# A fourth pair of recurrent output tiles by seven quarter products, in a planned one-core kernel

## The chip, the cores and the metric

The kernel runs on one core of one Trainium2 chip. The metric is the device time of one launch in microseconds (us): the time before is the median of three runs. A core has five engines that matter here, each with a queue of its own that it works through in order: TensorE (PE in the profile, with its weight loads as PEld), VectorE (DVE), ScalarE (ACT), GpSimd (POOL) and SyncE (SP). SP issues nearly all plain transfers; GpSimd issues the accumulating ones, in which the data that arrive are added to what stands at the destination.

## What is computed

One layer of a hybrid mixer, 1024 tokens by 1024 channels, all in float32. The reference, cut to what matters:

```python
h = rmsnorm(x, norm_g) * (1 + scale) + shift          # shift, scale, gate from c
u = h @ w_in                                          # 1024 x 5120
cv, cg, cs, lx, ls = split(u)                         # five blocks of 1024 channels

v = causal_depthwise_conv(cv * sigmoid(cg), dw_w, dw_b)      # 31 taps
v = silu(layernorm(v, cln_g, cln_b))
y_conv = (v @ pw2_w + pw2_b) * silu(cs)

xs = causal_depthwise_conv(lx, sc_w, sc_b)                   # 4 taps
r, i = sigmoid(xs @ wr + br), sigmoid(xs @ wi + bi)          # block-diagonal, 8 heads of 128
a = exp(-8 * r * softplus(-lam))
hs = linear_scan(a, sqrt(1 - a * a) * i * xs)
y_lru = hs * silu(ls)

x = x + (1 + gate) * (concat(y_conv, y_lru) @ w_out)
out = rmsnorm(x, final_g)
```

The change is in one part of one product: `y_lru @ w_out[1024:]`, called "lru output" below.

## The kernel before

**Layout.** Channels lie on the 128 partitions, tokens along the free axis. A 1024-channel array is eight tiles of 128 x 1024; for `y_lru` a tile is one head.

**Products in three terms.** A float32 product is made from rounded parts. ScalarE casts an operand to a high part (`whi`, `yh`, `vh…`), VectorE, GpSimd or an accumulating transfer makes the low part (`wlo`, `yl`, `vl…`), and TensorE adds three terms: high by high (H), low input by high weight (X), high input by low weight (W). For an lru weight the low part is made by `remainder`: ScalarE writes the negated high part, and a transfer issued by GpSimd adds the weight from DRAM onto it.

**Quarter products.** The two later matrices (the pointwise `pw2` and the upper half of `w_out`) are multiplied as 2 x 2 blocks with seven block products in place of eight. The blocks are two output tiles by two halves of the tokens, and heads or channel tiles are taken in twos. The operands of the seven are blocks (A11, A12, A22 of the weight; B11, B21, B22 of the input) and sums of blocks (S1 to S4, T1 to T4). `quarters` makes the input's operands out of full tiles, with VectorE and ScalarE. `lru_pair` does this for a pair of lru output tiles over heads 0 to 3 (`JS = (0, 1)`, two twos), and adds heads 4 to 7 in the ordinary way. The order of its products is `LORDER = "p1zy2q3s4r"`: `p` is heads 4 to 7 of the first tile into the PSUM tile `lp`, `q` and `r` are the halves of heads 4 to 7 of the second tile, the others are the seven quarter products. PSUM tile `lx` is read out several times between its products. Before the change pairs 0, 1 and 2 are made so (`LRU_P = 3`), and output tiles 6 and 7 are plain: eight heads, three terms, two halves of 512 tokens, in PSUM tile `ps`.

**Sums of weights.** `lru_prepare` makes S1 to S4 of a pair early in the program, by loads, negated copies and accumulating loads into `lz`, splits them into `lh` and `ll`, and stores both in DRAM. `lru_pair` loads them back (`lsh`, `lsl`). `lru_sums` makes the T operands over heads 0 to 3 (`yhs`, `yls`).

**Results.** Each lru output tile is scaled by the gate into an `acc` tile and added to a copy of the input in DRAM (`accd`) by an accumulating transfer; `fin` loads it back in the last stage.

**The planner.** The program's order isn't written out. Every operation is handed to `Plan` with an engine, a cost, a priority and its reads and writes; `Plan.order` simulates the engines, and on each engine starts the ready operation of lowest priority number for which buffers are free. What comes out is a fixed order for each engine. Priorities count in slots: `n` goes up by one for each output tile, the lru output has slots 40 to 47, the pointwise stage starts at `C0 = 48`, the output stage at `D0 = 56`. The constants at the head of the file shift priorities.

**Buffers.** `big` is a pool of 47 tiles of 128 x 1024 float32, used for nearly everything. `raw`, `whi` and `wlo` are pools of two such tiles each, for weights. Where `w_bufs` is given "big", the high and low parts come from `big`; before the change all eight lru weights do (`LWB = "big"`). A convolution result that is ready long before the layer norm can be parked: `SPILL` names the tiles that `conv_sum` stores in DRAM (`cd`) and loads back (`cr`).

**Lines that the prediction touches.** L541 is the matmul of `mm_k` (plain tiles, and `p`, `q`, `r` of a pair), L1400 the matmul of the quarter products in `lru_pair`, L717 that of the pointwise and output stages, L386 and L394 ScalarE's casts and other operations, L405, L413 and L427 VectorE's (L413 also GpSimd's), L418 the accumulating transfers, L432 SP's transfers. Most are lines of helpers, so groups are told apart by the names of the tiles.

Of the kernel before, what the change touches and what calls it, by code (L numbers as in the profile page):

```python
# [14 lines left out]
P = 128  # L15
D = 1024
T = 1024
KT = D // P
# [28 lines left out]
UK = 7  # L47
HRES = 2
POOLED = (1, 3, 5)
TLATE = 2.5  # L50
QGATES = ((1, 5), (3, 0), (3, 2), (3, 4))
OUT_P = (0, 1, 2, 3)
HELD = (1, 2, 3)
# [23 lines left out]
NP = {0: (6, 0, 1), 512: (6, 0, 7), 768: (6, 0)}  # L77
SUMS = (2, 0, 4, 3, 1, 6, 7, 5)
CSD = 2
SPILL = (0,2,4)  # L80
SPP0, SPP1, SPN = 30, 40.5, 39
EVN = 4
CQR = 2
YHEADS, YSLOT = 2, 36
JS = (0, 1)
LRU_P = 3
NJ = len(JS)
LK = tuple(2 * j + z for z in (0, 1) for j in JS) + tuple(k for k in range(KT) if k // 2 not in JS)
LACT = ((0, 0), (0, 1), (1, 0), (1, 1))
LORDER = "p1zy2q3s4r"  # L90
LTP = 0.5
LTD = (2,1)
PREN, PRES = 5, 3
PREP, XCP = 18, 19
# [1 line left out]
XCN = 33  # L96
LEV = ()
LWB = "big"
LWO = 0.5
FINP = -0.5  # L100
BCLATE = False
BEHIND = 0
TERMS = {**{("pw2_0", c): ("HW", "X") for c in "1z"}, **{(f"out_{p}", "1"): ("HX", "W") for p in (0, 1, 2, 3)}, **{(f"pw2_{p}", "1"): ("HX", "W") for p in (1, 2, 3)}}
LTERMS = {}
LLATE = 45
SLOTT = {46: ("HX", "W"), 47: ("HX", "W")}
FINQ = 0.0
LRV = ()
# [48 lines left out]
class Plan:  # L157
# [14 lines left out]
    @staticmethod  # L172
    def keys(items):
        for it in items:
            if isinstance(it, tuple):
                yield it
            else:
                for i in range(it.parts):
                    yield (it, i)
# [162 lines left out]
def hymba_layer(ctx: ExitStack, tc: tile.TileContext, xT, vecs, mod_w, w_first, w_in,  # L342
# [37 lines left out]
    def ACT(prio, out, in_, func, n=T, bias=None, scale=None, accum=None, r=(), w=(),  # L380
            reserve=0, after=()):
        kw = {}

        def emit():
            if func == "copy":
                act.copy(out(), in_())  # L386
                return
            if bias is not None:
                kw["bias"] = bias
            if scale is not None:  # L390
                kw["scale"] = scale
            if accum is not None:
                kw["accum_out"] = accum
            act.activation(out=out(), in_=in_(), func=func, **kw)  # L394
        ptr = sum(x is not None and not isinstance(x, float) for x in (bias, scale))
        return S.op("ACT", a_cost(n, ptr) + (0.1 if accum is not None else 0), emit, prio, r, w,
                    table=SETS.get(func), reserve=reserve, after=after)
# [121 lines left out]
    def w_bufs(s, where=None):  # L519
        n = number[s]  # L520
        raw[s] = S.buf("raw", f"raw{n}", F32, KT)
        if where == "all":
            raw[s] = S.buf("big", f"raw{n}", F32, KT)
        whi[s] = S.buf("big" if where else "whi", f"whi{n}", F32R, KT)
        wlo[s] = S.buf("big" if where else "wlo", f"wlo{n}", F32R, KT)
# [285 lines left out]
    for i in range(IDLE):  # L811
        if i == IDLE0:
            for z in (0, 1):
# [3 lines left out]
             after=[spread_op] if i >= IDLE0 else [])  # L817
# [44 lines left out]
    for i, ld in enumerate(LOADS):  # L862
        p = due[ld] = i - 100.0
        k = int(ld[1])
# [4 lines left out]
        elif ld[0] in "wW":  # L869
            nk = 1 + (ld[0] == "W")  # L870
            rw, hi, lo = fw[k - k % 2]
# [492 lines left out]
    def lru_pair(p, n, use, firsts):  # L1364
        rest = LK[2 * NJ:]
        s0, s1 = ("lru", 2 * p), ("lru", 2 * p + 1)
        q = n - 1.4 - LWO
        for s in (s0, s1):
            w_bufs(s, LWB)
            DMA(n - 2.5 - LWO, k3(raw[s]), lambda s=s: wsrc(s)[:, :, :], FULL_BYTES, w=[raw[s]])  # L1370
        r0, r1 = raw[s0], raw[s1]
        for s, k in ((s0, 0), (s1, NJ)):
            hi, lo, r = whi[s], wlo[s], raw[s]
            cut = lambda b, k=k: (lambda: k3(b)()[:, k:, :])
            keys = lambda b, k=k: [(b, i) for i in range(k, KT)]
            ACT(q, cut(hi), cut(r), "copy", (KT - k) * P, r=keys(r), w=keys(hi))
            if s[1] in LRV:
                SUB(q, "DVE", cut(lo), cut(r), cut(hi), (KT - k) * P, r=keys(r) + keys(hi), w=keys(lo))
            else:
                remainder(q, cut(lo), cut(hi), lambda s=s, k=k: wsrc(s)[:, k:, :], (KT - k) * P, keys(hi), keys(lo))  # L1380
        def kk(b, i):
            return [(b, k) for k in range(i * NJ, i * NJ + NJ)]

        sh, sl = (big_buf(f"ls{h}{p}", F32R) for h in "hl")
        for h, t in zip("hl", (sh, sl)):
            DMA(n - 2.2, lambda t=t: t().bitcast(F32), lambda h=h: s_d[h, p], FULL_BYTES, r=[("ls", h, p)], w=[t], after=firsts)
        wq = {"S3": (sh, sl, 0, 0), "S4": (sh, sl, 1, 0), "S2": (sh, sl, 2, 0), "S1": (sh, sl, 3, 0),
              "A11": (whi[s0], wlo[s0], 0, None), "A12": (whi[s0], wlo[s0], 1, None),
              "A22": (whi[s1], wlo[s1], 1, None)}
        p0, x, y = mm_tile(f"lp{p}"), mm_tile(f"lx{p}"), acc_tile(f"ly{p}")  # L1390
        g, ops = 0.0, {}

        def quarter(c, a, b, ps, h, begin):
            wh, wl, i, key = wq[a]
            rk = [(wh, key), (wl, key)] if key is not None else kk(wh, i) + kk(wl, i)
            for j, (bh, bl) in enumerate(lsets[b]):
                def emit(j=j, bh=bh, bl=bl):
                    o = (i * NJ + j) * P
                    for lhs, rhs, t in ((wh, bh, 0), (wh, bl, 1), (wl, bh, 2)):
                        pe.matmul(half(ps, h)(), lhs()[:, o:o + P], half(*rhs)(),  # L1400
                                  start=begin and j == 0 and t == 0, stop=j == NJ - 1 and t == 2,
                                  skip_group_check=True)
                o = S.op("PE", 3 * (H + 32) / 2400, emit, n + g, [*rk, bh, bl],
                         [(ps, h if ps.parts > 1 else 0)], columns=3 * H)
                ops.setdefault(c, o)

        for c in LORDER:
            g += 0.12
            if c == "p":
                groups = LTERMS.get(p, ("HXW",))  # L1410
                for gr in groups:
                    for k in rest:
                        o = mm_k(n + g, p0, s0, yh, yl, k, FULL, first=rest[0], group=gr,
                                 end=gr == groups[-1])
                        ops.setdefault(c, o)
            elif c == "q":
                for k in rest:
                    mm_k(n + g, y, s1, yh, yl, k, FULL[1:], off=H, first=-1)
                use(n, 1, 1, half(y, 0), (y, 0))
            elif c == "r":  # L1420
                for k in rest:
                    mm_k(n + g, x, s1, yh, yl, k, FULL[:1], first=-1)
                use(n, 1, 0, half(x, 0), (x, 0))
            else:
                a, b, ps, h, begin, i, z = {
                    "1": ("A11", "B11", x, 0, True, 0, 0), "z": ("A12", "B21", p0, 0, False, 0, 0),
                    "2": ("S2", "T2", x, 0, False, 0, 1), "3": ("S3", "T3", x, 0, False, 1, 1),
                    "y": ("S1", "T1", y, 0, True, 0, 1), "s": ("S4", "B22", p0, 1, False, 0, 1),
                    "4": ("A22", "T4", x, 0, False, None, 0)}[c]
                quarter(c, a, b, ps, h, begin)  # L1430
                if i is not None:
                    use(n, i, z, half(ps, h), (ps, h if ps.parts > 1 else 0))
        return ops["p"], ops["2"]
# [67 lines left out]
    for s in slots[4:]:  # L1501
# [5 lines left out]
        if s[0] == "pair":  # L1507
            ts = [big_buf(f"acc{m}", parts=2) for m in (2 * s[1], 2 * s[1] + 1)]
            begun = set()

            def use(n, i, h, ps, key, s=s, ts=ts, begun=begun):
                m, to, tk = 2 * s[1] + i, half(ts[i], h), (ts[i], h)
                if (i, h) not in begun:
                    begun.add((i, h))
                    if (i, h) in LACT:
                        ACT(n + 0.5, to, ps, AF.Copy, H, scale=gate1[:, m:m + 1], r=[key, ("gate1", m)], w=[tk])
                    else:
                        TS(n + 0.5, to, ps, gate1[:, m:m + 1], None, ALU.mult, r=[key, ("gate1", m)], w=[tk], n=H)
                    return
                STT(n + 0.5, to, ps, gate1[:, m:m + 1], to, ALU.mult, ALU.add, H,  # L1520
                    r=[tk, key, ("gate1", m)], w=[tk])
            started[n], started[n + 1] = lru_pair(s[1], n, use, [started[n - 2]])
            for m, t in zip((2 * s[1], 2 * s[1] + 1), ts):
                acc_store(n, m, t)
            n += 1
            continue
        if s not in NEXT:
            if s[0] == "lru":
                weights(s, n=n - LWO, eng="DVE" if s[1] in LRV else "DMA", where=LWB,
                        later=[started[LLATE]] if LLATE else [])  # L1530
            else:
                weights(s, late=[pending_evac[n]] if n in pending_evac else ())
# [243 lines left out]
```

## Time and profile before

| | us |
|---|---|
| median of three runs | 727.45 |
| lowest, highest | 727.34, 728.15 |
| the profiled execution, its own time | 728.6 |
| its span, first to last instruction | 726.8 |
| TensorE busy in the span | 717.4 |
| VectorE busy | 616.5 |
| ScalarE busy | 481.0 |
| GpSimd busy | 170.9 |

The granted TensorE clock was 0.996 of full speed over the span. A row of a group of instructions reads: line, engine, operation, output from inputs, shape, count; then the busy time and the mean ns of one; then the engine's idle time ahead of them and what ended it. A row of waits reads: who waited, for whom, us in total, times, longest. A row of the chain reads: start, us, what; a row of the timeline: start, us, engine, line, operation. Busy times of TensorE overlap, since matmuls are pipelined. Rows of transfers give the count, the size of one, and the median us from issue to landing. In a row of a stretch each engine has its busy us and, in brackets, its instructions.

### The profile page before, as it was taken

Reading aid. Unit: us, or ns where it says so; the run is one execution under the profiler, and the core shown is the slowest. Engines: PE = TensorE matmul, PEld = TensorE weight load, DVE = VectorE, ACT = ScalarE, POOL = GpSimd, SP = SyncE. Lnnn points to the kernel's source line nnn. Section 1 sums busy time; section 2 is a strip of 40 time slices with the busy share of each in tenths; the row PEclk is TensorE's granted clock in tenths of the full one; section 3 lists DMA queues with packets and bytes.
Section 4 is the critical chain, followed back from the end, with each engine's and each line's share of the span. In section 5 each row is a group of like instructions: output and inputs, shape, how many; then the busy total and the mean of one; then the engine's idle time right before and its main releaser. Section 6 shows DMA issues by size and latency. Waiting matters only on the chain.

```text
span 726.8 us, 9080 instructions
## 1 busy us (share of the span) xinstructions
PE 717.4 (99%) x3274; PEld 596.6 (82%) x3274; DVE 616.5 (85%) x848; ACT 481.0 (66%) x615; POOL 170.9 (24%) x172
## 2 busy tenths in 40 slices
PE   8999999999999999999999999999999999999996
PEld 7888888888888888888888888878888888888885
DVE  6999999889779999689499985999779766999646
ACT  7650679654779767966949779868785345745322
POOL 0035223343534230232220220111120101100003
PEclk9999999999999999999999999999999999999998
DMA  9946338758798998799999587998856946774006
GB/s 337 407 150 181 51 95 231 209 118 199 168 222 196 272 227 215 178 221 216 192 203 319 106 174 168 260 234 245 195 94 109 287 112 137 235 187 178 25 15 216
DMA packets 46059, 137.80 MB, mean 190 GB/s; under 512 B 5200, under 2 KB 15824, under 8 KB 45904
## 3 DMA queue, kind: packets, MB, share of 16 engines
q0 software_dynamic: 20016, 54.84, 42.0%
q1 hardware_dynamic: 24992, 81.48, 32.1%
q10 hardware_dynamic: 1008, 0.92, 0.4%
q8 instruction: 25, 0.41, 0.2%
q14 instruction: 18, 0.15, 0.1%
HBM read 79.37 MB, written 21.50 MB: 139 GB/s over the span
## 4 chain that ended last, share of the span: by engine, by line
PE 88%; ACT 4%; DVE 3%; issue 2%; DMA 1%; SPq 0%; DVEq 0%; ACTq 0%
PE ps L541 50%; PE xout L717 6%; PE xpw L717 6%; PE first L848 5%; PE ypw L717 3%; PE gate L1268 2%; PE lp L541 2%; PE lx L1400 2%; PE y L687 2%; PE zout L717 1%; PE zpw L717 1%; PE ly L541 1%; PE lx L541 1%; PE yout L717 1%; PE lp L1400 1%
## 5 line engine op out<-in xcount | busy, mean ns | idle before, releaser
L541 PE MATMUL ps<-uh,whi 128*128 128x512 f32 x576 | 177.4, 389 | 0.0
L541 PE MATMUL ps<-ul,whi 128*128 128x512 f32 x576 | 177.3, 389 | 0.0
L541 PE MATMUL ps<-uh,wlo 128*128 128x512 f32 x576 | 177.3, 389 | 0.0
L541 PEld LDWEIGHTS ps<-ul,whi 128*128 128x128 f32 x576 | 108.1, 188 | 22.5
L541 PEld LDWEIGHTS ps<-uh,wlo 128*128 128x128 f32 x576 | 108.1, 188 | 22.4
L541 PEld LDWEIGHTS ps<-uh,whi 128*128 128x128 f32 x576 | 108.0, 188 | 22.4
L386 ACT CAST whi<-raw 128x1024 fp32r<-128x1024 f32 (+1 forms) x44 | 45.1, 1031 | 44.1 <-PE ps L541 27.7
L418 POOL DMA_DIRECT2D es<-cq x45 | 41.0, 911 | 128.3 <-ACT cq L394 81.9
L413 POOL TENSOR_TENSOR wlo<-raw,whi 128x1024 fp32r<-128x1024 f32 x16 | 41.6, 2606 | 89.8 <-ACT whi L386 89.6
L394 ACT ACT_TABLE_LOAD x45 | 57.7, 1283 | 6.2 <-issue 2.5
L405 DVE SCALAR_TENSOR_TENSOR cacc<-v,V,cacc 128x511 f32<-128x511 f32 (+14 forms) x75 | 55.6, 741 | 0.5
L405 DVE SCALAR_TENSOR_TENSOR caccs<-v,V,caccs 128x511 f32<-128x511 f32 (+6 forms) x70 | 52.0, 743 | 2.2 <-ACT caccs L394 1.1
L405 DVE SCALAR_TENSOR_TENSOR caccs<-c,wsum,caccs 128x511 f32<-128x511 f32 (+6 forms) x70 | 52.0, 742 | 0.8
L418 POOL DMA_DIRECT2D oo<-co x39 | 37.0, 980 | 45.3 <-issue 11.9
L394 ACT ACTIVATE cq<-v,V 128x511 f32<-128x511 f32 (+14 forms) x45 | 31.7, 707 | 0.0
L405 DVE SCALAR_TENSOR_TENSOR modw<-modw,sc 128x1024 f32<-128x1024 f32 x23 | 29.5, 1286 | 2.1 <-DMA modw<-in_mod_w_dram 2.1
L405 DVE SCALAR_TENSOR_TENSOR xs<-ps,V,xs 128x1023 f32<-128x1023 f32 (+2 forms) x24 | 30.6, 1275 | 0.0
L413 DVE TENSOR_TENSOR wlo<-raw,whi 128x1024 fp32r<-128x1024 f32 x20 | 24.4, 1219 | 6.5 <-ACT whi L386 6.3
L394 ACT ACTIVATE cq<-c,wsum 128x512 f32<-128x512 f32 x42 | 29.6, 712 | 0.0
L394 ACT ACTIVATE co<-v,V 128x510 f32<-128x510 f32 (+12 forms) x39 | 26.9, 706 | 0.0
L394 ACT ACTIVATE finsq<-fin 128x512 f32<-128x512 f32 (+2 forms) x14 | 7.9, 570 | 27.6 <-DVE fin L405 14.4
L413 POOL TENSOR_TENSOR o<-fin,bc 128x256 f32<-128x256 f32 (+1 forms) x8 | 7.8, 996 | 68.1 <-ACT bc L386 68.1
(413 smaller groups left out, 1582.2 us busy)
## 6 DMA issues: line engine op xcount, KB each, us to landing
raw<-in_w_in_dram SPq DMA_DIRECT2D x36, 512.0 KB, 5.8
modw<-in_mod_w_dram SPq DMA_DIRECT2D x24, 512.0 KB, 9.2
scsd<-scs SPq DMA_DIRECT2D x8, 512.0 KB, 4.5
raw<-in_w_out_dram SPq DMA_DIRECT2D x8, 512.0 KB, 7.7
accd<-acc POOLq DMA_DIRECT2D x8, 512.0 KB, 7.3
rawpw<-in_pw_dram SPq DMA_DIRECT2D x8, 512.0 KB, 4.6
scsr<-scsd SPq DMA_DIRECT2D x8, 512.0 KB, 4.5
rawout<-in_w_out_dram SPq DMA_DIRECT2D x8, 512.0 KB, 3.5
```

The source lines that it names most:

```text
L386: act.copy(out(), in_())
L394: act.activation(out=out(), in_=in_(), func=func, **kw)
L405: dve.scalar_tensor_tensor(out=out(), in0=in0(), scalar=scalar, in1=in1(), op0=op0, op1=op1, accum_out=accum)
L413: lambda: e.tensor_tensor(out=out(), in0=a(), in1=b(), op=op), prio, r, w,
L418: return S.op("POOL", ISSUE, lambda: pool.dma_start(out(), a(), accum_op=ALU.add), prio, r, w, lag=RATE * n / T, after=after, flight=flight)
L541: pe.matmul(ps()[:, a - off:b - off], k3(lhs)()[:, at, :], rhs[k]()[:, a:b], start=(k == first and lhs is wh and rhs is xh and (a - off) % ...
L687: pe.matmul(to(), half(*lhs)()[:, j * P:j * P + P], half(*rhs)()[:, c0:c1], start=a == "S1" and j == 0 and t == 0, stop=j == KT // 2 - 1 a ...
L717: pe.matmul(half(ps, 0)(), half(*lhs)()[:, j * P:j * P + P], half(*rhs)(), start=start and at == 0 and i == 0, stop=at == len(order) - 1 a ...
L848: pe.matmul(ps()[:, a - off:b - off], fw_part(lhs, k, i * P, i * P + P)(), rhs()[:, a:b], start=k == 0 and lhs is wh and rhs is xh, stop=k ...
L1268: pe.matmul(ps()[:, c0:c1], lhs()[:, j, :], rhs()[:, c0:c1], start=st == 0, stop=st == 2)
L1400: pe.matmul(half(ps, h)(), lhs()[:, o:o + P], half(*rhs)(), start=begin and j == 0 and t == 0, stop=j == NJ - 1 and t == 2, skip_group_che ...
```

## The change

The fourth pair (output tiles 6 and 7) is made by `lru_pair` too, so no plain lru tile is left. The plain path's constants (`SLOTT`, `LLATE`) have no user any more. With it go seven settings:

- `SPILL`: convolution tiles 0 and 2 are parked, tile 4 stays in `big`.
- `LWBS`: lru weights 4 to 7 take their high and low parts from `big` as before; weights 0 to 3 take them from the two fixed buffers of `whi` and `wlo`.
- `LTERMS`: in pairs 1, 2 and 3 product `p` runs its H and X terms over all four heads first, then the W terms.
- `LTP` from 0.5 to 0: the head sums have a lower priority number, by half a slot.
- `LWO` from 0.5 to 0.7: the loads and splits of lru weights too, by 0.2 of a slot.
- `TLATE` from 2.5 to 3.0: the T operands in `quarters` have a higher one, by half a slot.
- `LSN = 2` and `LWG = 0` are new names, at values that give the code of before.

```diff
-TLATE = 2.5
+TLATE = 3.0
...
-SPILL = (0,2,4)
+SPILL = (0, 2)
...
-LRU_P = 3
+LRU_P = 4
...
-LTP = 0.5
+LTP = 0.0
...
-LWO = 0.5
+LWO = 0.7
...
+LSN = 2
+LWBS = (4, 5, 6, 7)
+LWG = 0
...
-LTERMS = {}
+LTERMS = {p: ("HX", "W") for p in (1, 2, 3)}
...
         for s in (s0, s1):
-            w_bufs(s, LWB)
+            w_bufs(s, LWB if s[1] in LWBS else None)
...
-            ACT(q, cut(hi), cut(r), "copy", (KT - k) * P, r=keys(r), w=keys(hi))
+            ACT(q, cut(hi), cut(r), "copy", (KT - k) * P, r=keys(r), w=keys(hi),
+                after=[started[n - LWG]] if LWG and p else [])
...
-            started[n], started[n + 1] = lru_pair(s[1], n, use, [started[n - 2]])
+            started[n], started[n + 1] = lru_pair(s[1], n, use, [started[n - LSN if s[1] else n - 2]])
...
-                weights(s, n=n - LWO, eng="DVE" if s[1] in LRV else "DMA", where=LWB,
+                weights(s, n=n - LWO, eng="DVE" if s[1] in LRV else "DMA",
+                        where=LWB if s[1] in LWBS else None,
```

## The prediction

> **What bounds the kernel now.** I read the page first, then who waited for whom with TensorE alone, then the chain of work that ended last.
>
> ```profile
> span 726.8 us, 9080 instructions
> PE 717.4 (99%) x3274; PEld 596.6 (82%) x3274; DVE 616.5 (85%) x848; ACT 481.0 (66%) x615; POOL 170.9 (24%) x172
> PE token_stats L805 <- DVE ones L463: 1.1, 1, 1.1
> PE finbc L770 <- DVE rs65.7_0_5820 L779: 0.9, 1, 0.9
> PE first L848 <- DVE ul L405: 0.8, 1, 0.8
> PE lp L541 <- DVE yl L413: 0.3, 1, 0.3
> ```
>
> TensorE is busy in 99% of the span, and its four waits add up to 3.1 us. Three stand at the two ends of the program; only the last, 0.3 us, stands in the middle, at the first matmuls of the first lru pair (the row says: a low half `yl` came late from VectorE). The chain says the same:
>
> ```profile
> 475.63 2.60 PE lp L541 x10
> ...
> 541.01 19.04 PE ps L541 x84
> 560.05 2.72 PE xpw L717 x12
> ...
> 721.07 1.57 DVE o L405 x4
> ```
>
> From 475.63 on it never leaves TensorE until the final scaling. So whatever leaves TensorE's queue between 475 and 717 is worth its whole length, and whatever makes TensorE wait there costs its whole length: nothing behind it has slack. The 84 matmuls of 128x512 took 19.04 us, 0.2267 us each.
>
> **What the change removes.** lru output tiles 6 and 7 are plain tiles now. Their rows, and those of their evictions beside those of a pair:
>
> ```profile
> L541 PE MATMUL ps<-yl,whi 128*128 128x512 f32 x32 | 9.9, 389 | 0.0
> L541 PE MATMUL ps<-yh,whi 128*128 128x512 f32 x32 | 9.9, 389 | 0.0
> L541 PE MATMUL ps<-yh,wlo 128*128 128x512 f32 x32 | 7.6, 389 | 0.0
> L427 DVE TENSOR_SCALAR acc<-ps,gate 128x1024 f32<-128x1024 f32 x2 | 2.6, 1278 | 0.1
> L405 DVE SCALAR_TENSOR_TENSOR acc<-lx,gate,acc 128x512 f32<-128x512 f32 x2 | 1.5, 745 | 0.0
> ```
>
> 3 x 32 = 96 matmuls. A pair is, by the code, heads 4 to 7 in full (24 into `lp`, 12 + 12 for the second tile) and seven quarter products over two head pairs with three terms each (7 x 2 x 3 = 42): 90. TensorE loses 6 matmuls, 6 x 0.2267 = **1.36 us**. That is 0.19% of the time, and it is all that the change can take off by itself.
>
> VectorE loses two evictions (2.6 us) and gets four of 0.745 us (3.0 us): +0.4 us. ScalarE gets four half evictions, which a pair has beside VectorE's; I take them at about VectorE's 0.745 us, 3.0 us, and it loses a quarter of two casts and two negated copies. Both lie beside TensorE if there is room; that room is the subject of the second rival.
>
> **What it adds early.** The block sums for pair 3, made between 60 and 133 us. Those of pairs 0 to 2:
>
> ```profile
> L418 POOL DMA_DIRECT2D lz<-in_w_out_dram x12: 853/887/1232, 64.9 to 107.3; - x12
> L394 ACT ACTIVATE lz<-lz x9: 397/401/420, 64.1 to 99.0; 128x256 f32<-128x256 f32 x9
> L386 ACT CAST lh<-lz x3: 1038/1041/1053, 110.4 to 118.4; 128x1024 fp32r<-128x1024 f32 x3
> L418 POOL DMA_DIRECT2D ll<-lz x3: 859/859/879, 118.0 to 123.4; - x3
> ```
>
> One more pair is a third of it: 3 x 0.40 + 1.04 and a negated copy of about the same 1.04 = 3.3 us of ScalarE, 5 accumulating loads of 0.87 us = 4.3 us of GpSimd's queue, and on SP's queue one load, two stores, and later two loads before the pair. The work that hides it is the projection's matmuls, on which TensorE waited for nothing while three such sets were made. I take 0. If the cover were gone, a low weight half that GpSimd makes would be late by at most the 4.3 us of issues; bounds 0 and 4.3. One parked conv tile fewer removes a store and a load of 512 KB, off the path: 0.
>
> **What it moves.** (a) The weights of lru tiles 0 to 3 leave the `big` pool for the two fixed `whi`/`wlo` buffers that the projection uses until its end. They can be cast only when TensorE has let go of a buffer. The rows that price this:
>
> ```profile
> 461.56 0.82 ACT L386 CAST whi<-raw 128x768 fp32r<-128x768 f32 x1
> 463.67 0.87 POOL L418 DMA_DIRECT2D wlo<-in_w_out_dram  x1 [2.86 <-ACT wlo L394]
> wlo<-in_w_out_dram POOLq DMA_DIRECT2D x1, 384.0 KB, 8.6
> wlo<-in_w_out_dram POOLq DMA_DIRECT2D x1, 384.0 KB, 7.4
> wlo<-in_w_out_dram POOLq DMA_DIRECT2D x1, 384.0 KB, 9.7
> 471.32 0.61 PE L541 MATMUL lp<-yh,whi 128*128 128x512 f32 x2
> 480.26 0.39 PE L541 MATMUL ly<-yh,wlo 128*128 128x512 f32 x1
> 493.67 0.62 PE L541 MATMUL lp<-yh,whi 128*128 128x512 f32 x2
> 505.69 0.39 PE L541 MATMUL ly<-yh,wlo 128*128 128x512 f32 x1
> ```
>
> From the cast of tile 1's weight to the issue of its low half are 463.67 - 461.56 = 2.11 us, and the landing took 8.6 us (7.4 and 9.7 for tiles 3 and 5): 10.7 us in all, 9.5 to 11.8. Tile 1's buffer comes free when the last projection tile ends, at 471.32, where the first pair begins. So its low half is there at 482.0 (480.8 to 483.1), and TensorE first wants it at 480.26: 1.8 us late (0.5 to 2.9). Between stand products of the first pair that don't need it and that now come after it: the second half of product 2 (3 matmuls) and product z (6), 9 x 0.2267 = 2.0 us. Which comes first is the planner's choice, and its flight time for such a load is 6.0 (`LAND`), under all three rows. Tile 3's buffer comes free at 493.67; ready at 504.4 (503.2 to 505.5), wanted at 505.69: in time, by 0.2 us at worst. Tile 2's buffer is free once z is done, and the new order of its terms puts the low half last, behind 16 matmuls (3.6 us). I take 0 for the whole, since for each of the three the cover is the larger number at the middle landing; bounds 0 and 2.9 us. Behind a late weight are queued, on TensorE, all the later products of the pair, and with them every matmul to the end.
>
> The Trainium skill's page "DMA: Bandwidth & Descriptors", section "Anatomy of one DMA — SWDGE (gpsimd) path", fits such a load as 2.0 us plus its bytes over 436 GB/s; an estimate from that is 2.9 us for 384 KB. By that rule tile 1's weight would be five us early and the first rival below would have no chance. The trace disagrees (7.4 to 9.7 us), so the rows above decide.
>
> (b) `LTP` lets the sums over heads 0 to 3 go earlier, `LWO` the loads by 0.2 of a slot, `TLATE` the T operands half a slot later.
>
> ```profile
> 471.30:493.60 22.30, 21.91 (x95) 17.45 (x94) 21.39 (x27) 14.57 (x19) 3.48 (x4) 1.00 0.94 254
> 540.80:559.80 19.00, 19.00 (x85) 15.72 (x85) 18.89 (x26) 10.98 (x14) 3.52 (x4) 1.00 0.54 85
> ```
>
> In the first pair's stretch 95 matmuls (21.54 us) took 22.30: 0.8 us is lost there, in which VectorE (21.39 of 22.30) is the engine that sets the pace. Another order can win up to 0.8 or lose as much again; I take 0, as VectorE's work there stays the same.
>
> **The sum.** 1.36 + 0 + 0 + 0. The profiled execution took 728.6 us, 726.8 of span and 1.8 around it; it becomes 727.2. It lies 1.15 above the median of the three runs, which becomes 727.45 - 1.36 = **726.1**.
>
> **Rivals.** *The fixed buffers eat it.* TensorE waits for tile 1's, or tile 3's, low half. For it: the planner's 6.0 against 7.4 to 9.7. Against: the 2.0 us of other products. Price 0.6 to 2.8 us, time 726.7 to 728.9, middle 727.8.
>
> *The pool squeeze, which ends slower.* `big` has 47 buffers, and it is full when the operands of the pointwise stage are made:
>
> ```profile
> DVE vla L413 <- DMA accd<-acc: 3.4, 1, 3.4
> DVE vla L413 <- PE lx L1400: 2.0, 1, 2.0
> 561.21 1.21 DVE L413 TENSOR_TENSOR vlc<-vt,vhc 128x1024 fp32r<-128x1024 f32 x1
> 567.59 0.39 PE L717 MATMUL xpw<-vlc,h34pw 128*128 128x512 f32 x1
> ```
>
> VectorE's split `vla` neither reads `acc` nor an `accd` load; that it waited for that store can only be for its buffer. With a fourth pair, the eight buffers of the head sums and two of loaded block sums live on through the stretch 540.8 to 559.8, in which VectorE is busy for 18.89 of 19.00 us with just these operands. What it can't make there comes later, and the pointwise stage begins 1.36 us sooner. The last `vlc` is ready at 562.42 and wanted at 567.59: 5.2 us, 3.8 after the change. So it decides from 3.8 us of VectorE idle on. The idle of today (3.4 + 2.0 = 5.4) once more costs 1.6 us; if the work of 12 us is put off, 8.2. Middle 4.9: 726.1 + 4.9 = 731.0; from 6.6 us of idle on the kernel is slower than before by over 0.2%. Against it: four to eight weight buffers leave the pool, though before this stretch, and the pointwise weights' sums no longer wait for the start of tile 7.
>
> *The new order also wins the 0.8 us of the first pair*: 725.3. For it, sums that come sooner; against it, VectorE's share.
>
> *It does less than it says*: `LSN` and `LWG` change nothing at their values, and 90 for 96 is certain by the code. No chance.
>
> **Numbers.** The saving alone 0.42 (725.7 to 726.6), with the first pair's gaps 0.12, fixed buffers 0.20, pool squeeze 0.26. A change of 0.2%, 1.45 us, is about what a measurement of this kernel can tell from none: faster is under 726.0, which halves the first case. Faster 0.21 + 0.12, and a little for waits that vanish elsewhere: 0.35. Slower, above 728.9: nearly all of the squeeze, 0.24. Same 0.41. The range goes from 724.9 (the first pair's gain and half a us of spread) to 731.0, the middle of the squeeze; that leaves out its dearer half, 0.13, and the early bound of 4.3. The likeliest case's own range is 725.7 to 726.6.
>
> **What would show it.** 3268 matmuls in place of 3274, and TensorE's waits still at some 3 us, with the pointwise stage's first matmul near 558.7 in place of 559.89: the forecast. A wait of a `ly` matmul for a `wlo` load near 482 or 505: the first rival. A wait of an `xpw` or `zpw` matmul for VectorE between 558 and 572, with VectorE idle before 558 on a store or a release: the second. A new TensorE wait before 135 us would show the early work wrongly priced. I am wrong altogether if TensorE's waits grow and yet the time falls, or if the time falls by more than 2.2 us.

## The result, and the profile after

The kernel after takes 729.48 us (median of 21 runs, 728.42 to 730.26); the kernel before, beside it, 727.97 (21 runs, 727.10 to 729.54). The ratio is 1.0019, with a 95% interval of 1.0013 to 1.0026: the change costs some 1.4 us where 1.4 us less was forecast. The time lies inside 724.9 to 731.0, but not on the side that was forecast.

The page of the profile after, its first lines, and who waited for whom with TensorE alone (us in total, times, longest):

```profile
span 727.5 us, 9081 instructions
PE 716.5 (98%) x3268; PEld 596.5 (82%) x3268; DVE 616.5 (85%) x850; ACT 484.2 (67%) x623; POOL 174.8 (24%) x177
PE lx L1404 <- ACT acc L397: 1.6, 1, 1.6
PE lx L1404 <- DMA yls<-sls: 1.1, 1, 1.1
PE token_stats L808 <- DVE ones L466: 1.1, 1, 1.1
PE finbc L773 <- DVE rs65.7_0_5839 L782: 0.9, 1, 0.9
```

The six matmuls are gone (3268 for 3274). The waits at the two ends stand as before; in the middle the 0.3 us for `yl` has gone, and two waits are new, both on `lx` in a pair's second quarter product.

Single executions also differ in their start, so I compare a stretch. First and last mark of it, in the timeline (start, us, engine, line, operation), with the first plain projection matmul ahead of them; the kernel before:

```profile
56.27 0.61 PE L541 MATMUL ps<-uh,whi 128*128 128x512 f32 x2
702.82 1.02 PE L764 MATMUL finbc<-ones,finss 128*128 128x1 f32 x8
```

and the kernel after:

```profile
55.69 0.61 PE L544 MATMUL ps<-uh,whi 128*128 128x512 f32 x2
470.71 0.39 PE L1404 MATMUL lx<-yh,whi 128*128 128x512 f32 x1
703.47 1.02 PE L767 MATMUL finbc<-ones,finss 128*128 128x1 f32 x8
```

From 56.27 to the first lru matmul at 471.32 the kernel before takes 415.05 us, the one after 415.02: that part takes as long as it did, and the 0.6 us between the two executions was there at 56 us. From the first lru matmul to the statistics of the final norm, before takes 231.50 us, after 232.76: **+1.26 us**; the medians of the kernels differ by 1.5. "Stretch" below means this interval. It is read from the one profiled execution of each kernel, whose own time lay up to 1.4 us from its kernel's median (3.5 us in the row "held back, the same").

**The first wait.** TensorE, and the accumulating transfer it waits for, after:

```profile
473.65 0.87 POOL L421 DMA_DIRECT2D wlo<-in_w_out_dram  x1 [6.91 <-DVE yl L416]
476.20 0.86 POOL L421 DMA_DIRECT2D yls<-sls  x1 [1.68 <-ACT yls L397]
...
484.31 0.39 PE L1404 MATMUL lx<-yhs,lsh 128*128 128x512 f32 x1
485.81 0.50 PE L1404 MATMUL lx<-yls,lsh 128*128 128x512 f32 x1 [1.11 <-DMA yls<-sls]
486.15 0.39 PE L1404 MATMUL lx<-yhs,lsl 128*128 128x512 f32 x1
```

`yls` is the low part of the second sum of heads 2 and 3. From 484.31 to 486.15 two matmuls take 1.84 us instead of 0.45: 1.39 us lost. The transfer was issued at 476.20 and landed 9.6 us later; in the kernel before the two such transfers were issued at 469.97 and 472.82 and landed in 5.0 and 4.6.

**The second wait**, in the fourth pair:

```profile
541.66 0.87 POOL L421 DMA_DIRECT2D accd<-acc  x1 [8.18 <-ACT acc L397]
...
543.44 0.39 PE L1404 MATMUL lx<-yh,whi 128*128 128x512 f32 x1
...
547.12 1.05 ACT L389 CAST vhc<-vt 128x1024 fp32r<-128x1024 f32 x1 [2.40 <-DMA accd<-acc]
548.59 0.68 ACT L397 ACTIVATE acc<-lx,gate 128x512 f32<-128x512 f32 x1
549.32 0.50 PE L1404 MATMUL lx<-yhs,lsh 128*128 128x512 f32 x1 [1.64 <-ACT acc L397]
```

Read it upwards. Product 2 may write `lx` only when product 1 has been read out. Product 1 (six matmuls from 543.44, done by 545) is read out by ScalarE only at 548.59, since ScalarE stood for 2.40 us in front of a cast, `vhc`, and then had this cast and one more to do. By the profile the store of tile 5's `acc`, issued at 541.66, ended that wait. The cast neither reads nor writes an `acc` or `accd`, so what it waited for can only be its place in the pool, the slot that this `acc` held until its store had landed; the kernel with one late cast, below, bears that out. Here 1.9 us are lost (1.64 and the slow restart).

### The profile page after: what moved, and what is told of

Read it like the earlier page. It is cut to its first block, busy times and chain, and to the rows that moved or that the text cites. A ratio compares the mean times of both kernels' runs of the same rounds, so it can differ in the third digit from the quotient of the medians.

```text
span 727.5 us, 9081 instructions
## 1 busy us (share of the span) xinstructions
PE 716.5 (98%) x3268; PEld 596.5 (82%) x3268; DVE 616.5 (85%) x850; ACT 484.2 (67%) x623; POOL 174.8 (24%) x177
## 4 chain that ended last, share of the span: by engine, by line
PE 90%; issue 3%; DVE 2%; DMA 2%; ACT 1%; POOL 0%; DVEq 0%; POOLq 0%; ACTq 0%
PE ps L544 50%; PE xout L720 6%; PE xpw L720 6%; PE first L851 5%; PE ypw L720 3%; PE gate L1271 3%; PE lx L1404 2%; PE y L690 2%; PE lp L544 1%; PE zout L720 1%; PE zpw L720 1%; DMA yls<-sls 1%; PE ly L544 1%; PE lx L544 1%; PE yout L720 1%
## 5 line engine op out<-in xcount | busy, mean ns | idle before, releaser
L389 ACT CAST xsh<-xs 128x1024 fp32r<-128x1024 f32 x8 | 8.4, 1051 | 23.9 <-DVE xs L408 16.9
```

## The experiments

My theories. **A**: the first wait is the transfer's long landing, stretched by SyncE's loads that run beside it. **B**: it is the late issue, behind weight 1. **C**: the second wait is ScalarE's queue, blocked by a cast without a slot. Each kernel is the kernel after with one edit or two, except the two with the fixed buffers, which keep the other settings of the kernel before; each time and ratio is against the kernel before in the same session.

| kernel | median, us | ratio (95%) | stretch, us |
|---|---|---|---|
| before | 727.9 to 728.1 | 1 | 231.50 |
| after | 729.48 | 1.0013 to 1.0026 | 232.76 |
| SyncE held back | 727.74 | 0.9986 to 1.0005 | 231.46 |
| `yls` by VectorE | 728.64 | 0.9997 to 1.0015 | 231.96 |
| one late cast | 728.85 | 1.0001 to 1.0018 | 232.42 |
| three pairs, new settings | 728.65 | 1.0000 to 1.0017 | 232.36 |
| the same with early sums | 729.25 | 1.0007 to 1.0024 | 231.94 |
| held back, two late casts | 728.41 | 1.0002 to 1.0019 | 231.50 |
| VectorE, one late cast | 727.27 | 0.9980 to 0.9997 | 230.94 |
| and a late subtraction | 727.81 | 0.9986 to 1.0003 | 230.82 |
| held back, the same | 727.03 | 0.9981 to 1.0003 | 234.28 |
| fixed buffers alone | 732.63 | 1.0043 to 1.0072 | 236.31 |
| pair and fixed buffers | 729.20 | 1.0006 to 1.0023 | 232.36 |
| `yls` ahead of weight 1 | 729.43 | 1.0009 to 1.0027 | 232.87 |

**SyncE's loads held back.**

```diff
+        if j == 1:
+            gated = dram.tile([1, 64], F32, tag="gated", name="gated")
+            S.gate = lambda: sp.dma_start(gated, lo()[0:1, 0:64].bitcast(F32))
...
+        gate = find("SP", "lsh1")
...
+            if o is gate:
+                self.gate()
             o.emit()
```

> The changed kernel with one tiny load (64 numbers of the low part of the summed heads) put into SyncE's queue ahead of the loads of the second pair's block sums, so that these and the five loads behind them start only when the low part has landed. Theory A (the low part lands 9.4 us after its issue because SyncE's loads of 475 to 482 us share the DMA engines with it): it lands about 5 to 7 us after its issue, TensorE's wait of 1.1 us in the first pair is gone, and the time falls by 1.0 to 1.3 us to about 728.3. Theory B (it is late because it is issued at 476.2, some 3.4 us later than before, behind the casts of weight 1): the landing stays near 9 us after the issue, the wait stays near 1.1 us and the time near 729.5; it may rise if the delayed loads come late themselves.

No TensorE wait is left in the first pair. Transfers issued from 470 to 486 us (count, size, median landing), after:

```profile
lsl<-lsdl SPq DMA_DIRECT2D x2, 512.0 KB, 11.1
yls<-sls POOLq DMA_DIRECT2D x1, 512.0 KB, 9.6
cr<-cd SPq DMA_DIRECT2D x1, 512.0 KB, 9.5
wlo<-in_w_out_dram POOLq DMA_DIRECT2D x1, 512.0 KB, 10.2
```

and with SyncE held back:

```profile
yls<-sls POOLq DMA_DIRECT2D x1, 512.0 KB, 7.4
wlo<-in_w_out_dram POOLq DMA_DIRECT2D x1, 512.0 KB, 5.5
lsl<-lsdl SPq DMA_DIRECT2D x1, 512.0 KB, 5.6
cr<-cd SPq DMA_DIRECT2D x1, 512.0 KB, 6.0
```

The same transfers, spread over a longer time, land in half to three quarters of the time each. `yls`, issued at 475.64, is there at 483.0, and the matmul that reads it runs at 483.98 without a wait. The stretch is 1.30 us shorter than after, as expected; the median is 1.7 lower, more than the 1.0 to 1.3 expected. Theory A holds for the landing, as far as 9.6 to 7.4 us, short of the 5 to 7 expected; the rest, down to the 4.6 of before, the loads held back don't explain. (The pair's first `yls`, issued at 465.88 in the kernel after, ahead of these loads, took 7.5.) The planner gives SyncE's loads a time, but in the program nothing holds one back except its place in SyncE's queue, a free slot and its data. After, SyncE issued a store and six loads shortly before and during the flight of `yls` (476.20 to 485.8); these are the first and the last:

```profile
474.88 0.32 SPq L435 DMA_DIRECT2D scsd<-scs  x1
...
482.04 0.80 SPq L435 DMA_DIRECT2D lsl<-lsdl  x1
```

**The low part by VectorE.**

```diff
+        S.low = lambda: dve.tensor_tensor(out=lo(), in0=x(), in1=hi().bitcast(F32), op=ALU.subtract)
...
+            if o is add:
+                self.low()
+            elif o is not neg:
+                o.emit()
```

> The changed kernel with the low part of the second summed head of heads 2 and 3 made by one VectorE subtraction (about 1.2 us) in the place of ScalarE's negated copy and the accumulating transfer. Both theories of the first stall (A and B) expect TensorE's wait on this tile in the first pair gone, and 1.0 to 1.3 us less: about 728.3. A rival (the wait only hides another one right behind it, VectorE's first evictions or weight 1's low half, which is due at about the same time) expects a wait of about the same size on the next operand and a time near 729.5.

The first pair's wait is gone, with nothing in its place, and the stretch is 0.80 us shorter; the median is 0.8 below after's, with overlapping spreads. Somewhat less than expected.

**`yls` ahead of weight 1** separates A from B.

```diff
+        first = [find("ACT", "sls3", "yhs11"), find("ACT", "yhs11", "yls11"), find("POOL", "yls11", "sls3")]
+        weight = find("ACT", "whi41", "wlo41")
...
+            if o is weight:
+                for x in first:
+                    place(x)
+                    x.emit()
+            place(o)
+            if o not in first:
+                o.emit()
```

> The changed kernel with ScalarE's cast and negated copy of the second summed head, and GpSimd's accumulating transfer of its low part, moved ahead of the negated copy and the transfer of weight 1's low half; nothing is held back or left out. Theory B (issue 3.4 us late, behind weight 1): the transfer is issued near 474, 2 us earlier, and even with a landing of 9 to 10 us it is there by 483.8, before its use at 484.5: no wait on it, and 0.5 to 1.3 us less, 728.2 to 729.0. Theory A alone (the landing stretches to whatever SyncE's loads leave): it still lands after 484.5 and the wait stays above 0.5 us. The rival (weight 1's low half, now 2 us later, takes its place): a wait of 0.5 to 2 us at the first matmul of the second tile that needs it, near 483, and 729.0 to 730.5.

The transfers of 470 to 486 us, TensorE's waits, and the timeline of TensorE:

```profile
yls<-sls POOLq DMA_DIRECT2D x1, 512.0 KB, 5.2
wlo<-in_w_out_dram POOLq DMA_DIRECT2D x1, 384.0 KB, 8.2
...
PE lx L1418 <- ACT acc L411: 1.6, 1, 1.6
PE ly L558 <- DMA wlo<-in_w_out_dram: 1.2, 1, 1.2
...
483.50 0.50 PE L558 MATMUL ly<-yh,wlo 128*128 128x512 f32 x1 [1.19 <-DMA wlo<-in_w_out_dram]
```

Issued at 474.26, 1.6 us before the first of SyncE's loads (475.90), `yls` lands in 5.2 us; weight 1's low half, issued at 475.25, now takes 8.2 (6.1 in after) and is 1.2 us late, at the place my first rival named. For `yls` itself theory B was right, there is no wait on it; A alone, by which it would still land after 484.5, was not. But nothing is won, 729.43 for 729.48, where B expected 728.2 to 729.0: the rival's wait takes the place of the old one. So issue time alone is no cure. As I read it, two accumulating transfers and SyncE's loads want the DMA engines at once (their mean busy share was 1.05 from 480 to 490 us in the kernel after), and the one that comes late pays. Taking one out (VectorE) or moving the others (held back) helped; changing the order didn't.

**One late cast.**

```diff
+    S.touch = lambda t: pool.memset(t, 0.0)
...
+        cast, low = find("ACT", "vt0", "vhc0"), find("DVE", "vt0", "vhc0", "vlc0")
...
+            if o is cast:
+                self.touch(cast.bufs[1]().bitcast(F32)[:, 0:1])
+            elif o is not low:
+                o.emit()
+            if o is second:
+                cast.emit()
+                low.emit()
```

`touch` claims the cast's slot in the old place; `second` is VectorE's eviction of the fourth pair's product 2.

> The changed kernel with one cast and its subtraction (vhc and vlc of the first pair of heads of the pointwise stage) moved behind the fourth pair's second eviction into the same tile, and their buffer claimed by GpSimd in the old place, so that every tile keeps its slot up to there. Theory C (the fourth pair's stall of 1.8 us is ScalarE standing in that cast, which waits for the store of tile 5, with the eviction that TensorE needs behind it): the eviction starts within about 0.5 us of its product's end, the wait at 549 us is gone, and the time falls by 1.5 to 1.8 us to about 727.8. The rival (the fourth pair's evictions are late whatever stands ahead, since product 2 follows product 1 too closely) expects a wait of 1 us or more at the same matmul and a time near 729.3.

ScalarE in the fourth pair, GpSimd's store of tile 5 and its claim of the slot, and TensorE's waits:

```profile
546.40 0.68 ACT L414 ACTIVATE acc<-lx,gate 128x512 f32<-128x512 f32 x1
546.98 1.03 ACT L406 CAST vhb<-c 128x1024 fp32r<-128x1024 f32 x1
...
542.49 0.87 POOL L438 DMA_DIRECT2D accd<-acc  x1 [8.17 <-ACT acc L414]
...
547.98 0.10 POOL L389 MEMSET vhc<- 128x1 f32 x1 [2.20 <-DMA accd<-acc]
...
PE lx L1421 <- DMA yls<-sls: 1.6, 1, 1.6
PE lx L1421 <- DVE acc L425: 0.8, 1, 0.8
```

The read-out comes 2 us sooner and product 2 no longer waits: theory C holds. The claim of the slot, an operation that does nothing but write into the cast's tile, now waits for the same store, 5.5 us after its issue. But 0.8 us comes back before product 4, whose tile VectorE reads out only behind another operand split (`vlc`) of the pointwise stage. In this execution the first wait was 1.6 us (`yls` landed in 10.1), so the stretch shows only 0.34 of the gain; the median is 0.6 below after's, not the 1.5 to 1.8 expected.

**The two cures together.** With VectorE's subtraction and one late cast:

> The subtraction on VectorE for the summed heads' low part, and only the first of the two late casts. A and C: the first pair without wait, the fourth with the 0.8 us before the fourth product that the late cast alone left: 728.6 less 0.9, about 727.7. The rival (the two gains do not add) expects 728.3 or more.

727.27 us, better than after by 2.2 and than before by 0.7, with an interval wholly below 1, and 0.4 below the 727.7 expected; of its waits in the stretch only the 0.8 before product 4 is left. With SyncE held back, and cast and subtraction of the second heads moved as well:

> The tiny load that holds SyncE's loads back until the summed heads' low part has landed, together with the late casts; here the cast and subtraction of the second pair of pointwise heads (vhc and vlc) are moved as well, behind the fourth pair's third eviction into its shared tile, since with only the first moved that eviction kept 0.8 us of wait behind it. Theories A and C together (the pair's six matmuls, 1.4 us, are real, and two waits of 1.3 and 1.8 us eat them): no TensorE wait above 0.3 us from 471 to 560 us, and 726.4 to 727.0, about 1.5 us below the kernel before. The rival (the slot that is short always goes to somebody, and the wait shows up at the next one, in the pointwise stage) expects a new wait of 0.8 us or more after 557 us and a time of 727.7 or more, as with the tiny load alone.

No wait is left in the lru pairs, but the time is 728.41 and a new wait stands in the pointwise stage, as the rival said:

```profile
PE zpw L741 <- DVE vlb L437: 1.3, 1, 1.3
```

VectorE, held up by the later cast, makes `vlb` too late. Then the subtraction alone moved, with the low part by VectorE:

```diff
+        late = {find("DVE", "acc6", "lx3"): (find("ACT", "vt0", "vhc0"), find("DVE", "vt0", "vhc0", "vlc0")),
+                find("DVE", "acc7", "lx3"): (find("DVE", "vt1", "vhc1", "vlc1"),)}
```

> As the kernel with VectorE's subtraction and the first late cast, and on VectorE alone the second pair's subtraction (vlc) moved behind the fourth pair's third eviction into its shared tile; its cast stays where it is. A and C: the 0.8 us before the fourth product go as well, no TensorE wait above 0.3 us between 471 us and the last block of the final normalisation, 0.6 to 0.8 us below that kernel's 727.27: 726.5 to 726.7. The rival (the missing slot comes out again in the pointwise stage, as it did when cast and subtraction were both moved) expects a wait there of 0.5 us or more and 727.3 or more.

> The same late cast and late subtraction, with the tiny load that holds SyncE's loads back in the place of VectorE's subtraction for the summed heads' low part. Theory A: as good as the other within 0.4 us, 726.4 to 726.9. The rival (the held-back loads arrive late for the second pair or the layer norm) expects a new wait between 490 and 530 us and 727.3 or more.

With the low part by VectorE:

```profile
PE xpw L741 <- DVE vlc L437: 0.2, 1, 0.2
```

The 0.8 us go, these 0.2 come, and the stretch is 0.12 shorter, not 0.6 to 0.8; where the rest went I did not find. The median, 727.81, is 0.5 higher: the rival's time was nearer, though its wait of 0.5 us isn't there. With SyncE held back the median is 727.03, close to the 726.4 to 726.9 expected and without a wait from 490 to 530 us, but its executions go from 726.42 to 730.57, and the profiled one, the slowest, shows what held that one up: a `yc` eviction stands behind a cast of a weight half that came late:

```profile
568.60 0.62 ACT L409 CAST hlpw<-rawpw 128x512 fp32r<-128x512 f32 x1 [1.70 <-DMA rawpw<-in_pw_dram]
...
571.32 0.50 PE L740 MATMUL ypw<-vhb,h34pw 128*128 128x512 f32 x1 [2.31 <-ACT yc L417]
```

That the loads held back earlier push this one was not tried apart.

**The parts alone.** Three pairs with the new settings, and the same with the fourth pair's sums made early and not used:

```diff
-LRU_P = 4
+LRU_P = 3
...
-            for p in range(LRU_P):
+            for p in range(4):
                 lru_prepare(p, [started[n]])
```

> The changed kernel's settings with three pairs in place of four (the last two lru tiles plain again, no early sums for the fourth pair). My prediction had the settings at nothing: 728.0, the time of the kernel before. Theory A/B/C: the first pair's stall of about 1.3 us is the settings' and stays, the fourth pair's is gone with the pair, the six matmuls come back (1.4 us): about 729.3 against 729.5, that is, the settings alone cost 1.0 to 1.3 us over the kernel before.

> The changed kernel's settings with three pairs, as before in this study, but with the fourth pair's block sums formed and stored at 60 to 133 us all the same, and then not used. My prediction's term for this early work is nothing (bounds 0 to 4.3 us): no TensorE wait between 55 and 140 us beyond those of the settings alone, and 728.65 within 0.5 us. The rival (its loads and adds push the projections' weights or the gate loads back) expects waits there and 729.3 or more.

The settings alone: 0.86 us more in the stretch than before, at two waits:

```profile
PE lx L1404 <- DMA wlo<-in_w_out_dram: 0.8, 1, 0.8
PE lx L1404 <- DMA yls<-sls: 0.2, 1, 0.2
```

Another mix than theory A/B expected (`yls` landed in 7.9 us here), of the same kind. The median is 0.6 above before, at the edge of the interval, and less than the 1.0 to 1.3 expected. With the early sums TensorE waits for nothing between 56 and 140 us; 56.11 to 471.14 us is again 415.03. The stretch is 0.4 shorter than without them; the median is 0.6 higher, just outside the 0.5 expected, and the intervals of the two overlap. The sums themselves cost nothing that the trace shows; where the 0.6 comes from stays open.

The fixed buffers alone, and with the pair, on the settings of before:

```diff
-TLATE = 3.0
+TLATE = 2.5
-SPILL = (0, 2)
+SPILL = (0, 2, 4)
-LTP = 0.0
+LTP = 0.5
-LWO = 0.7
+LWO = 0.5
-LTERMS = {p: ("HX", "W") for p in (1, 2, 3)}
+LTERMS = {}
```

(and `LRU_P = 3` for the buffers alone)

> The kernel before with one part of the change alone: the first four lru weights in the fixed buffers (three pairs, three parked conv tiles, the other settings as before). My prediction's term is nothing (bounds 0 to 2.9 us): 728.0 within 0.4. Its first rival expects TensorE to wait 0.5 us or more for a weight's low half near 471 to 482 or near 505 us, and 728.5 to 730.9.

> The kernel before with the fourth pair and the fixed buffers, but three parked conv tiles, the sums' order and the groups of products as before. My prediction (pair -1.4 us, buffers nothing) expects 726.6 to 727.0. Theory C (the fourth pair's own evictions stand behind casts that wait for a slot) expects a TensorE wait of 0.8 us or more between 535 and 560 us here too, and 727.5 or more. No wait there means that parking two tiles and not three makes the squeeze, and not the pair.

The buffers alone are the dearest kernel of all, 4.5 us above before and beyond both forecasts. Its waits, and its stretches of time (us, TensorE busy and matmuls, granted clock, DMA share, GB/s):

```profile
PE ly L544 <- DMA wlo<-in_w_out_dram: 2.0, 1, 2.0
PE ly L1404 <- DVE yls L416: 0.8, 1, 0.8
...
500.00:505.00 5.00, 5.00 (x23) 1.00 1.03 237
505.00:510.00 5.00, 3.05 (x11) 0.90 1.06 264
510.00:515.00 5.00, 5.00 (x25) 0.76 0.72 189
```

The 2.0 us stand at 507.62, where tile 3's low half is wanted: issued at 497.24, landed 10.3 us later. The 0.8 us stand at 474.92, for the low part of a head sum that VectorE makes. With the pair added no weight is late, and no `yls` either (the two transfers are issued at 466.83 and 468.73), but two evictions by VectorE are, 1.1 us before a matmul of `lp` at 548.50 and 0.7 before product 4; ahead of the first, VectorE stood in front of a `vla` as ScalarE did of `vhc`:

```profile
PE lp L1404 <- DVE acc L408: 1.1, 1, 1.1
PE lx L1404 <- DVE acc L408: 0.7, 1, 0.7
...
546.50 0.69 DVE L416 TENSOR_TENSOR vla<-cr,vha 128x512 fp32r<-128x512 f32 x1 [2.07 <-DMA accd<-acc]
```

So the squeeze comes with the pair, through either engine that evicts, and three parked tiles don't lift it. 727.5 or more was theory C's forecast; my prediction's 726.6 to 727.0 is missed by over 2 us.

## Why the prediction was wrong

- **Six matmuls, 1.36 us: right.** 3268 are left. The held-back kernel shows it in the stretch: 231.46, of which 2.0 us are its one wait (1.8 us at the same place as after's second, and the restart). Without it 229.4, 2.1 less than before: 1.36, and some 0.7 that the third rival had given to the first pair's gaps, whose wait for VectorE is gone indeed.
- **Early work, 0: right** (415.0 us three times).
- **"Both lie beside TensorE if there is room": this step failed for ScalarE's evictions.** A pair's evictions aren't work beside TensorE; they are links in its chain, product 1, eviction, product 2 into the same tile. A plain tile has none, so before the same wait for a slot (3.4 us of `vla` on the `accd` store) cost nothing. I had counted the four evictions by their 0.7 us and not by what stands ahead of them in ScalarE's queue. Measured: 1.9 us.
- **The pool squeeze: right place, wrong path and price.** I sent it through VectorE's late operands into the pointwise stage (4.9 us). It went through ScalarE's queue into the pair itself. In the repaired kernels the path I had described appears too, at 0.2 to 1.3 us.
- **(b), "I take 0, as VectorE's work there stays the same": this step failed too.** I priced the new order by the engine that was busiest, and didn't follow the one transfer in the first pair that the new order moves, `yls`, 3.4 us later and into six loads and a store. Measured: 1.4 us. The delay comes with the new settings: it is there with three pairs (issue at 476.03), and with the pair and the fixed buffers alone it isn't (468.73). Which of `LTP`, `LWO`, `TLATE`, `SPILL` and `LTERMS` brings it was not tried.
- **(a), 0: right for the change, for the wrong reason.** Tile 1's low half was issued at 473.65 and landed in 6.1 us, 479.8, wanted at 482.72: better than the 482.0 I gave it. Tile 3's was issued at 499.73 and landed in 8.4, 508.1, wanted at 508.46: 0.3 us of cover, with the start of the pair itself late. Taken alone the same buffers cost 4.5 us, above my bound of 2.9, with the largest wait, 2.0 us, at a matmul that the first rival had named. Landing times were the unknown, and I took their middle (8.6) where the cover was the size of their spread. One reading was wrong, with nothing resting on it: a landing of 2.9 us would have tile 1's low half ready at 476.3, 3.9 us early and not five.

The whole: 1.36 and 0.7 saved, 1.4 and 1.9 lost, +1.2; measured +1.26. What was not tried: which of the other settings, or the pair itself, gives the fixed buffers their cover in the change.

## What to carry to other kernels

When a product is split into parts that share an accumulator, put each eviction on the critical path and look at what stands ahead of it in its engine's queue: an operation that waits for a buffer blocks it, though the two have nothing to do with each other. Price a transfer by how many others are in flight at that time, and where two late ones compete, take one out rather than reorder them. A plan's order across queues is a wish; only a dependence holds a load back.

## What the runs showed of the hardware

- The landing of one and the same accumulating transfer of 512 KB, the second `yls` of the first pair: 4.6 us before (5.0 for the first), 5.2 with 1.6 us of head start over SyncE's loads, 7.4 with them held back, 7.9, 9.6 and 10.1 beside them. In the last four TensorE's wait followed it: 0, 0.2, 1.1, 1.6 us.
- Each of the two waits of the kernel after cost TensorE some 0.27 us beyond its idle time (1.39 for 1.11, 1.91 for 1.64): the first matmul behind it takes 0.50 us for 0.39, and the overlap with its forerunner (0.39 at a pitch of 0.2267) is lost.
- Waits of 1.11 to 1.77 us left the granted clock at 1.00. Those of 1.95 and 2.31 us were followed by 0.90 and 0.76, and by 0.72 and 0.94 in stretches of 5 us, and the matmuls behind them then stood 0.43 us apart for some 3 us, in place of 0.2267; in the kernel with the fixed buffers alone, whose stretch is 4.8 us longer than before with 2.8 us of idle time in it, this is most of the rest. The rows of the 2.31:

```profile
570.00:575.00 5.00, 3.68 (x10) 0.72 0.77 138
575.00:580.00 5.00, 5.00 (x22) 0.94 0.67 222
```

  The Trainium skill's page "TensorE: Matmul & The Clock Gate", Part 1, lets the clock fall after an idle window of about 3.4 us; here shorter waits were enough.
- Time less span, the median of a kernel's runs, was 1.8 us for before and after, and 2.4 for the kernel with the late subtraction: medians of two kernels can differ by 0.6 us with no difference in the trace.
